# A two-layer trunk on one core: where the attention's weight loads are issued, in which order its chunks of weights are split, and how far its scores run ahead

## The chip, the cores and the metric

The kernel runs on one core of a Trainium2 chip. The metric is the device time of one execution in microseconds (us). The engines of a core work on queues of their own and in order: TensorE (PE; PEld is its loading of stationary operands), VectorE (DVE), ScalarE (ACT), GpSimd (POOL) and SyncE (SP), which here only issues transfers. Each DMA is issued from the queue of one engine; those of SP and those of POOL are two different queues of transfers (q1 and q0 in the profile).

## The reference: what is computed

A sequence of 1024 tokens with 1024 features goes through two layers. Layer 0 mixes tokens with a gated linear recurrence (RG-LRU), layer 1 with stick-breaking attention; each is followed by a SwiGLU feed-forward network of width 2816, with RMS norms before each part, and one at the end. All values are float32. The part that the change is about is the attention, 16 heads of 64:

```python
z = jnp.einsum("bhqd,bhkd->bhqk", qb, kb).astype(jnp.float32) * scale
strict = s_idx < t_idx
log_fail = jnp.where(strict, jax.nn.log_sigmoid(-z), 0.0)
suffix = lax.cumsum(log_fail, axis=3, reverse=True) - log_fail
weights = jnp.where(strict, jnp.exp(jax.nn.log_sigmoid(z) + suffix), 0.0)
outs.append(jnp.einsum("bhqk,bhkd->bhqd", weights.astype(vb.dtype), vb))
```

A query's weight on a key is sigmoid(z) of that key times the product of sigmoid(-z) over all later keys before the query. The kernel forms F = sigmoid(-z) and scans it backwards with a running product: the difference of neighbouring products is the weight, so the products themselves are multiplied with differences of neighbouring rows of V.

## The kernel before, in words

The program is straight-line: Python loops write out every instruction once. Dense products keep float32 accuracy by splitting each operand into a high and a low part (a rounded copy made by ACT, and a subtraction made by DVE) and multiplying three times. A framework allocates the tiles of a pool (a tag with `bufs` buffers), places waits, and plans the order of instructions on an engine by its own costs, except inside `manual_schedule`, where the named engines keep the order in which the code is written. The attention section is written by hand for all five engines, SP among them. The feed-forward sections are written by hand for all but SP; there the planner orders SP's transfers, and it may set instructions of neighbouring sections between one another.

Attention works on pairs of heads (`q` = 0 to 7). One pair has 24 *chunks* of scores (`chunk_list`): 128 queries by up to 512 keys. For each chunk:

- `z_part` (L1646): two matmuls into a score bank of PSUM (`psZ`, two banks).
- `z_rest` (L1658): ACT's sigmoid into a tile `w` (three buffers; diagonal chunks of j >= 4 have tiles of their own).
- `scan` (L1665): DVE's backward running product, in place. A chunk that is not on the diagonal starts from the first column of the diagonal chunk of its queries.
- `turn_weights` (L1677): ACT's copy to float16 (`wx`, four buffers), DVE's subtraction for the low half, and a transposing DMA from SP into a tile `wt` (three buffers, each for four chunks).

`score` (L1774) does this a step at a time. It issues the matmuls of chunk c, then splits and turns chunk c-1 (`turn_weights`), then the sigmoid and the scan of chunk c. So ACT's order in a step is copy of c-1, sigmoid of c; DVE's order is subtraction of c-1, scan of c.

The main loop runs over `units` u (L1704: two matmuls each of turned weights with V, called av). Chunks are `LEAD` = 8 steps ahead of units. Each step has: a chunk's score, one entry of the list `later`, one unit, and two pieces of `fill`. Fill is the projection of the next pair's Q, K and V (`qkv_steps`): three *links* per pair, each 8 steps of 6 matmuls and an evacuation (`evacuate`) per 512 tokens. K's evacuation makes t on DVE, its high part on ACT and its low part on DVE, and POOL then issues the copies into `kk` (L1636). `later` holds short jobs that are served one a step: the split of the next link's weights (`next_weights`, L1548 and L1549), the squares and norms of V's columns (`column_norms`), and for a finished pair `gather`, `add_v` (a POOL addition, L1720, except for the last pair) and `parts` (ACT L1727 and DVE L1728, then two stores issued by POOL).

Weights of Q, K, V and of the output projection are loaded by `load_link`, one link ahead of their split. These loads go to POOL's queue, as two transfers of half a tile each (L121); all other weights are loaded by SP (L117), whole. They share three buffers `raw`. POOL's queue in attention thus holds, in order: weight loads, the copies of Q and K (L1632, L1633, L1636), additions, small integer work for the norms, a memset of one column of `vt` (L1594), and the stores and returns of finished rows. At the end of the last pair `bring_back` returns the stored rows in 26 transfers (L1513, L1514).

In the feed-forward sections `Weights.a_lo` (L716) subtracts for the low part of a weight tile, and `tasks` (L1124) lists at which position of the first visits the products that come back from memory are split (`split_op`).

Of the kernel before, what the change touches and what calls it, by code (L numbers as in the profile page):

```python
# [8 lines left out]
F32 = mybir.dt.float32  # L9
F32R = mybir.dt.float32r  # L10
BF16 = mybir.dt.bfloat16
# [6 lines left out]
P = 128  # L18
# [16 lines left out]
def trunk(  # L35
# [76 lines left out]

    def load_raw(src, shape, queue=nc.sync):
        raw = rp.tile([P, D], F32, tag="raw", name="raw")
        view = raw if len(shape) == 1 else raw.rearrange("p (a b) -> p a b", a=shape[0])
        if queue is nc.sync:
            queue.dma_start(view, src)  # L117
        else:
            for i in range(2):
                c = slice(i * D // 2, (i + 1) * D // 2)  # L120
                queue.dma_start(raw[:, c].rearrange("p (k c) -> p k c", c=P), src[:, 4 * i : 4 * i + 4])  # L121
        return raw
# [37 lines left out]
    class Mix:  # L160
# [7 lines left out]

        def load(self, i, **kw):
            self.raw[i] = load_raw(cols(self.src, self.order[i] * P), (ND,), **kw)  # L170

# [459 lines left out]
    def mix_out_ffn_in(mix, bias, layer, gnext, outs):  # L631
# [42 lines left out]
        class Weights:  # L674
# [40 lines left out]

            def a_lo(self):  # L716
                lo = wtile("wal")
                V.tensor_sub(self.full(lo), self.full(self.ra), self.full(f32(self.wa)))
                self.put((0, 1), self.wa, lo)
# [57 lines left out]
        with tc.manual_schedule(engines={E.PE, E.Activation, E.DVE, E.Pool}):  # L777
# [224 lines left out]
            for k, i in enumerate(ORDER0[:6]):  # L1002
                part(P0[i], w, i, rhs_in[i], (HK - 1,))
                if k == 1:
                    w.d_hi()
                    w.d_lo()
                elif k == 3:
                    nw.a_hi()
                elif k == 5:
                    nw.a_lo()  # L1010
                if k < 5:
                    post0(i, P0[i])
# [110 lines left out]
            L = NPROD  # L1123
            tasks = [(at, p, i) for at, i in zip((2, 2, 3, 4, 5, 5, L), ORDER) for p in range(2)]  # L1124

# [72 lines left out]
            for s_, (kind, x) in enumerate(steps):  # L1198
# [24 lines left out]
                for k, i in enumerate(ORDER):  # L1223
# [18 lines left out]
                    if not final and kind == "v" and x == NV - 1:  # L1242
# [5 lines left out]
                        elif k == 5:  # L1248
                            ql = ring.four.tile([P, D], F32R, tag="w", name="wlo")
                            V.tensor_sub(ql, raw, f32(qh))  # L1250
                            k3 = lambda t: t.rearrange("p (k c) -> p k c", k=ND)
                            wq0.append((k3(qh), k3(ql)))
# [234 lines left out]
    with ExitStack() as st:  # L1487
# [3 lines left out]
        psZ = pos.enter_context(tc.tile_pool(name="psZ", bufs=2, space=PSUM, side="right", reuse_waits="tile"))  # L1491
        psN = st.enter_context(tc.tile_pool(name="psN", bufs=1, space=PSUM, reuse_waits="tile"))
        psO = st.enter_context(tc.tile_pool(name="psO", bufs=2, space=PSUM, reuse_waits="tile"))
        psQ = qs.enter_context(tc.tile_pool(name="psQ", bufs=2, space=PSUM, side="right", reuse_waits="tile"))


        unit = ap.tile([P, NB], F32, name="unit")
        nc.gpsimd.memset(unit[:, 0 : NB - P], 0.0)
# [18 lines left out]
        def load_link(i):  # L1517
            q, which = divmod(i, 3)
            if q < NP:
                raws[i] = load_raw(cols(w_qkv, which * D + q * P), (ND,), queue=nc.gpsimd)  # L1520
            else:
                mix[0].load(which, queue=nc.gpsimd)

        def column_norms(raw, q):
            sq = ap.tile([P, ND, P], BF16, tag="sq", name="sq", bufs=1)
            r3 = raw.rearrange("p (k c) -> p k c", k=ND)

            def sums():
                nc.scalar.square(sq[:, 4:], r3[:, 4:])
                n_ps = psN.tile([P, 1], F32, tag="n", name="n_ps")  # L1530
                for k in range(ND):
# [11 lines left out]

            return lambda: nc.scalar.square(sq[:, 0:4], r3[:, 0:4]), sums

# [42 lines left out]
        def evacuate(q, which, n, ps):  # L1588
            full = lambda tag, m: [ap.tile([P, m, S], F32R, tag=tag, name=tag, bufs=4 if m == 1 else 3) for _ in range(2)]
            cs = slice(n * NB, (n + 1) * NB)  # L1590
            if which == 2:
                if n == 0:
                    VT[q] = ap.tile([P, S + 1], F32, tag="vt", name="vt", bufs=2)
                    nc.gpsimd.memset(VT[q][:, 0:1], 0.0)  # L1594
                    VV[q] = ap.tile([P, 2, NT, 2, HD], F16, tag="v", name="v", bufs=2)
                t = ap.tile([P, NB], F32, tag="t", name="t", bufs=2)
                after = VT[q][:, n * NB + 1 : (n + 1) * NB + 1]
                nc.vector.scalar_tensor_tensor(after, ps, f32(sv[q]), rbc[n], op0=ALU.mult, op1=ALU.mult)
                yield
                nc.vector.tensor_sub(t, VT[q][:, cs], after)  # L1600
                vx = ap.tile([P, 4, 2, P], F16, tag="vx", name="vx", bufs=1)
                t3 = t.rearrange("p (b c) -> p b c", b=4)
# [16 lines left out]
            else:  # L1619
                t = ap.tile([P, NB], F32, tag="t", name="t", bufs=2)  # L1620
                nc.vector.tensor_mul(t, ps, rbc[n])
# [24 lines left out]
        def z_part(q, hx, j, ci, c0, c1, diag):  # L1646
            nk = (j + 1) * P
            ps = psZ.tile([P, NB], F32, tag="z", name="z_ps")
            lhsT = Q[q][hx][:, j * P : (j + 1) * P]
# [27 lines left out]
        def turn_weights(q, hx, j, ci, c0, c1, diag):  # L1677
# [6 lines left out]
            if g not in T:  # L1684
                T[g] = ap.tile([P, 8, 4, P], F16, tag="wt", name="wt", bufs=3)
            nc.sync.dma_start(
# [9 lines left out]
        def av_part(q, hx, G, kb, first, last):  # L1696
# [42 lines left out]
            if hx == 1:  # L1739
                later.extend((add_v, parts))  # L1740

        heads = [(q, hx) for q in range(NP) for hx in range(2)]
        chunks = [c for q, hx in heads for c in chunk_list(q, hx)]
        units = [u for q, hx in heads for u in unit_list(q, hx)]
        LEAD = 8

# [131 lines left out]
```

## Time and profile before

| | us |
|---|---|
| median of 3 runs | 2302.44 |
| lowest and highest run | 2298.66 and 2302.54 |
| the profiled execution | 2293.64 |
| its span, first to last instruction | 2291.9 |
| PE busy in the span | 2137.0 (93%) |
| DVE busy | 1787.2 (78%) |
| ACT busy | 1135.0 (50%) |
| POOL busy | 261.1 (11%) |

Attention runs from about 952 to 1570 us of the span. A busy PE is not PE at its peak, since matmuls are pipelined; the granted clock (PEclk, 1.00 is full) tells how fast it was allowed to run. The DMA share is the mean over 16 engines of the time that packets took, and can pass 1 where transfers of two queues overlap. In rows of waits, the name on the right is what ended the wait; in a timeline, idle time before an instruction stands in brackets with what ended it.

### The profile page before, as it was taken

How to read it: one execution, taken by the hardware profiler on the slowest of the kernel's cores; microseconds unless marked ns; L12 is line 12 of the kernel's file. 1: busy time of each engine (PE TensorE's matmuls, PEld its weight loads, DVE VectorE, ACT ScalarE, POOL GpSimd, SP SyncE). 2: the span in 40 equal slices, each digit the busy share in tenths (PEclk: the TensorE clock that was granted, in tenths of full speed). 3: DMA queues.
4: the chain of work that ended last, by engine and by line, in shares of the span. 5: the costliest groups of instructions: out<-in, count | busy, mean ns of one | idle time of the engine just before them, and what ended most of it. 6: DMA issues, size and time to landing. Idle time of an engine off the chain costs nothing.

```text
span 2291.9 us, 28023 instructions
## 1 busy us (share of the span) xinstructions
PE 2137.0 (93%) x9838; PEld 1728.4 (75%) x9838; DVE 1787.2 (78%) x2604; ACT 1135.0 (50%) x1838; POOL 261.1 (11%) x334
## 2 busy tenths in 40 slices
PE   9999999999999999987778787649999999999999
PEld 7888888888888888865556555427888888888887
DVE  7888588888887888866668766645888888878886
ACT  6676445444444455644445544434454444444556
POOL 1222010000000000122222222231100000000002
PEclk9999999999999999998999999869999999999999
DMA  6111422344447745377878877796223444477452
GB/s 222 55 37 56 156 74 92 115 138 152 139 155 266 245 140 159 124 148 151 161 155 162 158 156 151 154 193 191 74 88 113 136 156 138 152 260 259 147 154 90
DMA packets 443981, 336.45 MB, mean 147 GB/s; under 512 B 187704, under 2 KB 356800, under 8 KB 443840
## 3 DMA queue, kind: packets, MB, share of 16 engines
q1 hardware_dynamic: 427168, 281.95, 43.6%
q0 software_dynamic: 16512, 52.44, 10.1%
q8 instruction: 77, 1.26, 0.2%
q14 instruction: 64, 0.52, 0.1%
q10 hardware_dynamic: 160, 0.27, 0.0%
HBM read 184.09 MB, written 83.36 MB: 117 GB/s over the span
## 4 chain that ended last, share of the span: by engine, by line
PE 73%; DVE 10%; issue 7%; ACT 5%; DMA 4%; POOL 2%; DVEq 0%; ACTq 0%
PE p_ps L150 16%; PE p_ps L148 16%; PE p_ps L149 16%; DMA wt<-wx 4%; DVE w L1670 3%; DVE w L1673 3%; PE a_ps L149 2%; PE a_ps L150 2%; PE a_ps L148 2%; PE ob_ps L149 2%; PE ob_ps L148 2%; PE ob_ps L150 2%; ACT wx L1681 2%; ACT w L1663 2%; DVE wx L1682 1%
## 5 line engine op out<-in xcount | busy, mean ns | idle before, releaser
L148 PE MATMUL p_ps<-vh,wbh 128*128 128x512 f32 x524 | 204.9, 391 | 0.0
L149 PE MATMUL p_ps<-vl,wbh 128*128 128x512 f32 x524 | 204.5, 390 | 0.0
L150 PE MATMUL p_ps<-vh,wbl 128*128 128x512 f32 x524 | 204.3, 390 | 0.3 <-DVE wbl L727 0.3
L148 PE MATMUL p_ps<-vh,wch 128*128 128x512 f32 x524 | 204.2, 390 | 0.0
L150 PE MATMUL p_ps<-vh,wcl 128*128 128x512 f32 x524 | 204.2, 390 | 0.0
L149 PE MATMUL p_ps<-vl,wch 128*128 128x512 f32 x524 | 203.9, 389 | 0.0
L1650 PE MATMUL z_ps<-kk,q 128*128 128x256 f32 (+1 forms) x192 | 78.2, 407 | 103.0 <-ACT w L1663 92.9
L1681 ACT CAST wx<-w 128x128 f16<-128x128 f32 (+1 forms) x192 | 97.9, 510 | 152.5 <-DVE w L1670 60.6
L1682 DVE TENSOR_TENSOR wx<-w,wx 128x128 f16<-128x128 f32 (+1 forms) x192 | 107.2, 558 | 75.7 <-ACT wx L1681 72.8
L723 ACT CAST wbh<-sb 128x1024 fp32r<-128x1024 f32 (+2 forms) x69 | 69.6, 1009 | 191.7 <-DVE sb L707 191.7
L150 PE MATMUL p_ps<-vh,wal 128*128 128x512 f32 x396 | 154.3, 390 | 0.1
L148 PE MATMUL p_ps<-vh,wah 128*128 128x512 f32 x396 | 154.1, 389 | 0.0
L149 PE MATMUL p_ps<-vl,wah 128*128 128x512 f32 x396 | 154.1, 389 | 0.0
L1650 PEld LDWEIGHTS z_ps<-kk,q 128*128 128x128 f32 x192 | 38.9, 202 | 133.4 <-ACT w L1663 117.4
L148 PE MATMUL qk_ps<-vh,whi 128*128 128x512 f32 x264 | 133.5, 506 | 0.0
L223 POOL TENSOR_TENSOR acc<-acc,rbc 128x512 f32<-128x512 f32 x30 | 40.7, 1357 | 772.5 <-ACT rbc L222 772.5
L121 POOL DMA_DIRECT2D raw<-in_attn_w_qkv x46 | 35.5, 771 | 752.3 <-DVE g L1186 623.2
L1663 ACT ACTIVATE w<-z_ps,rs 128x128 f32<-128x128 f32 (+1 forms) x192 | 110.5, 575 | 15.9 <-PE z_ps L1651 15.5
L1704 PE MATMUL av_ps<-wt,v 128*128 128x512 f16 (+3 forms) x384 | 104.4, 358 | 14.9 <-DMA wt<-wx 8.8
L150 PEld LDWEIGHTS p_ps<-vh,wbl 128*128 128x128 f32 x524 | 98.4, 188 | 22.3 <-DVE wbl L727 1.5
L150 PEld LDWEIGHTS p_ps<-vh,wcl 128*128 128x128 f32 x524 | 98.4, 188 | 21.0 <-DVE wcl L737 0.6
L148 PEld LDWEIGHTS p_ps<-vh,wch 128*128 128x128 f32 x524 | 98.4, 188 | 20.5 <-ACT tb L1182 0.2
(407 smaller groups left out, 6087.4 us busy)
## 6 DMA issues: line engine op xcount, KB each, us to landing
raw<-in_ffn_w_in SPq DMA_DIRECT2D x88, 512.0 KB, 4.0
vl<-pd SPq DMA_DIRECT2D x128, 256.0 KB, 3.6
pd<-U SPq DMA_DIRECT2D x90, 256.0 KB, 2.3
kk<-two POOLq DMA_DIRECT2D x64, 256.0 KB, 5.2
raw<-in_ffn_w_out SPq DMA_DIRECT2D x56, 256.0 KB, 3.8
raw<-in_attn_w_qkv POOLq DMA_DIRECT2D x46, 256.0 KB, 3.9
h<-hd SPq DMA_DIRECT2D x32, 256.0 KB, 5.3
hd<-h SPq DMA_DIRECT2D x32, 256.0 KB, 2.0
```

Of the source, the lines that this page charges most:

```text
L148: nc.tensor.matmul(ps, lhsT=wh, rhs=mh, start=first, stop=False, **kw)
L149: nc.tensor.matmul(ps, lhsT=wh, rhs=ml, start=False, stop=False, **kw)
L150: nc.tensor.matmul(ps, lhsT=wl, rhs=mh, start=False, stop=last, **kw)
L223: (eng or nc.gpsimd).tensor_add(acc[n], acc[n], sq)
L723: nc.scalar.copy(self.full(self.wb), self.full(self.sb))
L1650: nc.tensor.matmul(ps[:, 0 : c1 - c0], lhsT=lhsT, rhs=KK[q][hx][:, 0, c0:c1], start=True, stop=False)
L1663: nc.scalar.activation(F, ps[:, 0:n], AF.Sigmoid, scale=rs[:, j : j + 1])
L1670: nc.vector.tensor_tensor_scan(rev, rev, unit[:, NB - n :][:, ::-1], 0.0, op0=ALU.mult, op1=ALU.add)
L1673: nc.vector.tensor_tensor_scan(rev, rev, rev, first, op0=ALU.mult, op1=ALU.bypass)
L1681: nc.scalar.copy(wx[:, 0:m, 0], F)
L1682: nc.vector.tensor_sub(wx[:, 0:m, 1], F, wx[:, 0:m, 0])
L1704: nc.tensor.matmul(ps[:, q0 * P :], lhsT=lhsT, rhs=rhs, start=first and part == 0, stop=last and part == 1)
```

## The change

- `load_raw` always issues one whole transfer from SP; the two halves from POOL are gone, for the weights of Q, K, V and of the output projection.
- `score` issues matmuls, sigmoid and scan of chunk c first, and then splits and turns chunk c-1. In a step ACT's order is now sigmoid of c, copy of c-1; DVE's is scan of c, subtraction of c-1.
- Scores have four banks: a pool `psY` of two beside `psZ`, taken in turn. The bank of its own for the norms (`psN`) is gone; the norms take a score bank.
- `LEAD` is 10 instead of 8, and `wt` has four buffers instead of three.
- The squares of the norms (`sq`) and V's halves (`vx`) share the tag and the four buffers of `wx`. `t` has one buffer instead of two, and `unit`, an operand of the diagonal scans, is BF16 instead of float32.
- The two squares of the norms are two entries of `later` instead of the second being made right before the norm's matmuls; and an empty entry stands between `add_v` and `parts`.
- Outside attention: two subtractions for low parts are made in two pieces (the first weights of the second step of each feed-forward section, and the first weights of Q, there in the order in which the first link reads them), and two products are split one or two positions later in `tasks`.

```diff
-    def load_raw(src, shape, queue=nc.sync):
+    def load_raw(src, shape):
         raw = rp.tile([P, D], F32, tag="raw", name="raw")
         view = raw if len(shape) == 1 else raw.rearrange("p (a b) -> p a b", a=shape[0])
-        if queue is nc.sync:
-            queue.dma_start(view, src)
-        else:
-            for i in range(2):
-                c = slice(i * D // 2, (i + 1) * D // 2)
-                queue.dma_start(raw[:, c].rearrange("p (k c) -> p k c", c=P), src[:, 4 * i : 4 * i + 4])
+        nc.sync.dma_start(view, src)
         return raw
...
-            def a_lo(self):
+            def a_lo(self, parts=1):
                 lo = wtile("wal")
-                V.tensor_sub(self.full(lo), self.full(self.ra), self.full(f32(self.wa)))
+                if parts == 1:
+                    V.tensor_sub(self.full(lo), self.full(self.ra), self.full(f32(self.wa)))
+                else:
+                    for x in range(2):
+                        V.tensor_sub(self.part(lo, x), self.part(self.ra, x), self.part(f32(self.wa), x))
                 self.put((0, 1), self.wa, lo)
...
                 elif k == 5:
-                    nw.a_lo()
+                    nw.a_lo(2)
...
-            tasks = [(at, p, i) for at, i in zip((2, 2, 3, 4, 5, 5, L), ORDER) for p in range(2)]
+            tasks = [(at, p, i) for at, i in zip((2, 2, 3, 4, 5, L, L + 1), ORDER) for p in range(2)]
...
                             ql = ring.four.tile([P, D], F32R, tag="w", name="wlo")
-                            V.tensor_sub(ql, raw, f32(qh))
+                            ka = lambda t: t.rearrange("p (a k c) -> p a k c", a=2, k=HK)
+                            for y in (slice(1, 3), slice(0, HK, HK - 1)):
+                                V.tensor_sub(ka(ql)[:, :, y], ka(raw)[:, :, y], ka(f32(qh))[:, :, y])
...
-        psN = st.enter_context(tc.tile_pool(name="psN", bufs=1, space=PSUM, reuse_waits="tile"))
+        psY = st.enter_context(tc.tile_pool(name="psY", bufs=2, space=PSUM, reuse_waits="tile"))
+        taken = []
+
+        def z_bank(name):
+            taken.append(name)
+            return (psZ, psY)[len(taken) % 2].tile([P, NB], F32, tag="z", name=name)
...
-        unit = ap.tile([P, NB], F32, name="unit")
+        unit = ap.tile([P, NB], BF16, name="unit")
...
-                raws[i] = load_raw(cols(w_qkv, which * D + q * P), (ND,), queue=nc.gpsimd)
+                raws[i] = load_raw(cols(w_qkv, which * D + q * P), (ND,))
             else:
-                mix[0].load(which, queue=nc.gpsimd)
+                mix[0].load(which)
...
-            sq = ap.tile([P, ND, P], BF16, tag="sq", name="sq", bufs=1)
+            sq = ap.tile([P, ND, P], BF16, tag="wx", name="sq", bufs=4)
...
-                nc.scalar.square(sq[:, 4:], r3[:, 4:])
-                n_ps = psN.tile([P, 1], F32, tag="n", name="n_ps")
+                n_ps = z_bank("n_ps")[:, 0:1]
...
-            return lambda: nc.scalar.square(sq[:, 0:4], r3[:, 0:4]), sums
+            squared = lambda i: nc.scalar.square(sq[:, 4 * i : 4 * i + 4], r3[:, 4 * i : 4 * i + 4])
+            return lambda: squared(0), lambda: squared(1), sums
...
-                t = ap.tile([P, NB], F32, tag="t", name="t", bufs=2)
+                t = ap.tile([P, NB], F32, tag="t", name="t", bufs=1)
...
-                vx = ap.tile([P, 4, 2, P], F16, tag="vx", name="vx", bufs=1)
+                vx = ap.tile([P, 4, 2, P], F16, tag="wx", name="vx", bufs=4)
...
-            ps = psZ.tile([P, NB], F32, tag="z", name="z_ps")
+            ps = z_bank("z_ps")
...
-                T[g] = ap.tile([P, 8, 4, P], F16, tag="wt", name="wt", bufs=3)
+                T[g] = ap.tile([P, 8, 4, P], F16, tag="wt", name="wt", bufs=4)
...
             if hx == 1:
-                later.extend((add_v, parts))
+                later.extend((add_v, lambda: None, parts))
...
-        LEAD = 8
+        LEAD = 10
...
         def score(some):
-            ps = [z_part(*a) for a in some]
+            for a in some:
+                z_rest(z_part(*a), *a)
+                scan(*a)
             while turning:
                 turn_weights(*turning.pop(0))
-            for a in some:
-                z_rest(ps.pop(0), *a)
-                scan(*a)
-                turning.append(a)
+            turning.extend(some)
```

More of the change, by code (lines that the diff above doesn't have):

```diff
@@ L167, in __init__, with load @@
                 self.proc(i)
-        def load(self, i, **kw):
-            self.raw[i] = load_raw(cols(self.src, self.order[i] * P), (ND,), **kw)
+        def load(self, i):
+            self.raw[i] = load_raw(cols(self.src, self.order[i] * P), (ND,))
         def proc(self, i):
@@ L1619, in evacuate @@
             else:
-                t = ap.tile([P, NB], F32, tag="t", name="t", bufs=2)
+                t = ap.tile([P, NB], F32, tag="t", name="t", bufs=1)
                 nc.vector.tensor_mul(t, ps, rbc[n])
```

## The prediction

> **What bounds the kernel now.** First the page's head and the windows, to find the stage that loses time.
>
> ```profile
> span 2291.9 us, 28023 instructions
> ...
> core 0: us, PE busy (x) PEld busy (x) DVE busy (x) ACT busy (x) POOL busy (x), PEclk, DMA share, GB/s
> 160.00:900.00 740.00, 739.93 (x3433) 618.67 (x3432) 606.54 (x854) 358.64 (x539) 28.85 (x15) 1.00 0.45 144
> 1000.00:1500.00 500.00, 392.34 (x1735) 280.25 (x1733) 355.58 (x519) 244.35 (x478) 135.86 (x224) 0.92 0.80 156
> 1500.00:1570.00 70.00, 40.47 (x145) 24.40 (x145) 34.94 (x46) 22.72 (x43) 14.16 (x20) 0.73 0.97 183
> 1146.00:1216.00 70.00, 54.59 (x245) 39.08 (x244) 50.39 (x75) 34.46 (x68) 19.02 (x31) 0.95 0.79 158
> ```
>
> Outside attention PE is busy 739.93 of 740 us: nothing to win there. In 1000:1500 nobody is full: PE 392 of 500 us, DVE 356, ACT 244, DMA 0.80. One pair of heads (24 chunks of scores) lasts 70 us, with 50.4 us of DVE. So I read next who waits, engine by engine, in 1000:1500.
>
> ```profile
> engine line waited for: us in total, times, longest us
> DVE oo L1728 <- ACT oh L1727: 70.2, 7, 13.8
> DVE wx L1682 <- ACT wx L1681: 41.7, 61, 1.2
> DVE w L1673 <- ACT w L1663: 15.5, 7, 3.0
> DVE vx L1604 <- ACT vx L1603: 9.7, 14, 0.7
> ACT oh L1727 <- POOL oo L1720: 72.2, 7, 14.3
> ACT wx L1681 <- DVE w L1670: 51.4, 83, 1.7
> ACT wx L1681 <- DVE w L1673: 48.5, 42, 2.3
> PE z_ps L1650 <- ACT w L1663: 59.0, 30, 12.9
> PE n_ps L1532 <- ACT sq L1529: 25.3, 7, 4.5
> PE av_ps L1704 <- DMA wt<-wx: 8.8, 8, 1.6
> POOL raw L121 <- issue: 86.9, 23, 6.5
> ```
>
> DVE is idle for 500 - 355.6 = 144.4 us; its four rows add to 137.1. That is the whole account: DVE and ACT hold each other up, PE waits behind them (59.0). The timeline shows the two mechanisms.
>
> ```profile
> 1185.88 0.68 ACT L1663 ACTIVATE w<-z_ps,rs 128x512 f32<-128x512 f32 x1
> 1186.01 0.69 DVE L1682 TENSOR_TENSOR wx<-w,wx 128x512 f16<-128x512 f32 x1 [1.21 <-ACT wx L1681]
> 1186.62 1.28 DVE L1673 TENSOR_TENSOR_SCAN w<-w,w 128x512 f32<-128x512 f32 x1
> 1187.92 0.62 ACT L1681 CAST wx<-w 128x512 f16<-128x512 f32 x1 [1.37 <-DVE w L1673]
> ...
> 1189.04 2.44 POOL L1636 DMA_DIRECT2D kk<-two  x4 [9.31 <-ACT w L1663]
> 1192.92 0.79 POOL L121 DMA_DIRECT2D raw<-in_attn_w_qkv  x1 [1.44 <-issue]
> 1199.52 0.75 POOL L121 DMA_DIRECT2D raw<-in_attn_w_qkv  x1 [5.81 <-issue]
> 1200.29 1.10 POOL L1720 TENSOR_TENSOR oo<-oo,vt 128x512 f32<-128x512 f32 x1
> ...
> 1201.43 0.72 ACT L1727 ACTIVATE oh<-oo,av 128x512 fp32r<-128x512 f32 x1 [9.25 <-POOL oo L1720]
> ```
>
> Mechanism one: POOL's add sits in order behind a weight load whose second half gets out 5.81 us late, ACT stands 9.25 us before its scaling of that sum, and everything behind ACT stands too. Mechanism two: ACT's copy of chunk c-1 comes ahead of its sigmoid of chunk c, and needs the scan of c-1; so sigmoid, scan and copy run one after another (0.68 + 1.28 + 0.62).
>
> **The change, part by part.**
>
> *Loads to SyncE.* The add then follows its input, and gets one more step before ACT asks for it. Gain: the first DVE row, 70.2 us. The first pair has the same stall once, through the memset of vt behind a load:
>
> ```profile
> 992.64 0.75 POOL L121 DMA_DIRECT2D raw<-in_attn_w_qkv  x1 [5.78 <-issue]
> 993.38 0.12 POOL L1594 MEMSET vt<- 128x1 f32 x1
> ...
> 994.25 0.63 ACT L1603 ACTIVATE vx<-t 128x512 f16<-128x512 f32 x1 [6.54 <-DVE t L1600]
> ```
>
> That is 6.5 more. For this part a rule speaks against the gain. The Trainium skill (DMA: Bandwidth & Descriptors, section SWDGE vs HWDGE vs iDMA, "Issuing engines are not separate DMA queues") says that spreading issues over engines saves only the issuing time. By that rule these 77 us would not come back, since an issue is short. The trace disagrees: 86.9 us of waits before 23 POOL loads, none of them the 0.75 us of the issue itself.
>
> On SP the loads stand among the transposes. Their raw buffer was last read a link (8 steps) earlier, so SP does not wait for it; what is queued behind is transposes, costed below. At the start of the stage load 1 may fall behind the last stores of the residual on SP: between 0 and 5 us, I take 0, because the planner may place ACT's first split by arrival.
>
> *Split a scan later.* Sigmoid c no longer stands behind the scan of c-1, and copy c-1 finds its scan done. Gain at most the 41.7 us of the second DVE row. *Squares a step earlier and four banks:* PE reaches its norm matmuls with both halves squared, and scores can be four chunks ahead of the sigmoid; gain at most the 15.5 us of the third row (25.3 on PE are no path of their own). The 9.7 of vx stay. The new order's own needs: sigmoid c takes the w buffer of chunk c-3, which the subtraction of c-3 has freed a step earlier on DVE, so it does not wait; the norm's result takes one of the four score banks for a moment; and the four banks that the next section opens now come free with the last scores instead of standing empty, up to 1 us, which I leave at nothing. LEAD 10 adds two steps in which PE multiplies without new scores at the end and two without products at the start: the same instructions, spread otherwise.
>
> Sum of gains: 70.2 + 6.5 + 41.7 + 15.5 = 133.9 us.
>
> **What is late next.** Four things, each from a row:
>
> ```profile
> 1183.69 0.39 PE L1650 MATMUL z_ps<-kk,q 128*128 128x512 f32 x1
> ...
> 1191.72 0.39 PE L1650 MATMUL z_ps<-kk,q 128*128 128x512 f32 x1
> ACT two L1624 <- DVE t L1621: 29.5, 14, 2.3
> kk<-two POOLq DMA_DIRECT2D x56, 256.0 KB, 5.8
> raw<-in_ffn_w_in SPq DMA_DIRECT2D x88, 512.0 KB, 4.0
> DMA to landing us min/median/max: 2.3/4.0/8.5
> DMA to landing us min/median/max: 2.5/10.4/17.7
> ACT wx L1681 <- DMA wt<-wx: 32.0, 7, 11.9
> L1670 DVE TENSOR_TENSOR_SCAN w<-w,unit x114: 416/825/1227, 999.7 to 1498.0; 128x256 f32<-128x256 f32 x29, 128x384 f32<-128x384 f32 x29, 128x512 f32<-128x512 f32 x28, 128x128 f32<-128x128 f32 x28
> L718 DVE TENSOR_TENSOR wal<-raw,wah x70: 684/1218/1222, 307.6 to 2263.0; 128x1024 fp32r<-128x1024 f32 x58, 128x768 fp32r<-128x768 f32 x8, 128x512 fp32r<-128x512 f32 x4
> ```
>
> (The two landing lines are the transposed tiles wt, first in 1000:1480, then in 1490:1545; the wait for wt is that of 1000:1600; the scans are those of 1000:1500.)
>
> 1. K evacuations. ACT's cast waits for DVE's t in the same step, and the next sigmoid stands behind it: 0.62 + 0.68 = 1.3 us of DVE idle, 14 times: 18 us.
> 2. K's copies. Two issues of 2.44/4 each and 5.8 us to land, then score and sigmoid (0.39 + 0.68): 8.1 us before chunk 28, the first that reads the second half of the next pair's K, can be scanned. DVE has three steps of work until then, at 50.4/24 = 2.1 us each 6.3: 1.8 x 7 = 13 us.
> 3. PE. Four steps take 1191.72 - 1183.69 = 8.03 us, 24 take 48 us, against DVE's 50: two nearly full engines with three or four chunks between them. Between 0 and 3 us a pair, I take 1.5: 10 us.
> 4. Shared buffers. Squares and vx now take one of the four buffers of wx. From copy to landing it is 0.62 + 1.28 + 0.69 + 4.0 = 6.6 us; three buffers cover 3 x 2.1 = 6.3, four cover 8.4. Between 0 and 2 us a pair, I take 1: 7 us.
>
> Together 48 us come back. Net: 133.9 - 48 = 86 us.
>
> At nothing: LEAD 10 with four wt tiles (av waited 8.8 us in all, and the slack before an av goes from 4 steps to 6); the last pair, where the bringing back of stored rows floods the DMA and ACT waits for transposes (most of the 32.0 us) as before, between 5 us less and 10 more; unit in BF16, where no row shows a scan with a BF16 operand: 114 scans of about 0.825 us, 5% either way is 5 us, I take none; the split subtractions before the FFN (2 x 0.684 against 1.218, 0.15 us more DVE) and the splits of two products, one or two positions later, both under a PE that is never short there: up to 1 us if that cover went.
>
> The profiled execution took 2293.64 us around its 2291.9; the median of the runs is 2302.44, 8.8 more. 2293.64 - 86 = 2207.6, and against the median 2302.4 - 86 = **2216 us**.
>
> **The rivals.**
>
> *Floor.* Nothing comes back: 2302.4 - 134 = 2168. For it: POOL's add is the only long stall. Against: point 1 is in the order of the program.
>
> *DMA paces it.* At a share of 0.80, and if the mean cannot pass 0.90, 500 us shrink by 56: 2246. For it: 0.97 with DMA waits in 1500:1570. Against: there it is large transfers from one queue.
>
> *Loads ahead of transposes.* A transpose behind a load waits for it: it lands at 4.0 + 4.0 = 8.0 us, where four buffers at 2.1 us a step, less 2.6 for copy, scan and subtraction, cover 5.8. 2.2 us x 24 loads = 53: 2302.4 - 86 + 53 = 2269. The Trainium skill (DMA: Bandwidth & Descriptors, section Queues, rings and completion order) supports this: an engine takes turns between queues packet by packet, but serves one queue in its order, so a load loses its place beside the transposes and gets one ahead of them. No run so far shows it.
>
> *Loads not the cause.* Without the loads' 77 us: 134 - 77 - 48 = 9: 2293.
>
> *Slower.* The same place as the third rival, at the price of the flooded stretch: transposes behind each load land at 10.4 us, 4.6 over the cover, x 24 = 110 us: 2302.4 - 86 + 110 = 2326. It decides from a landing of 5.8 + 86/24 = 9.4 us on. For it: 10.4 was measured. Against: that took 26 transfers in a row, not one every 23 us.
>
> **How the numbers follow.** Forecast 0.48 (its own range 2185 to 2250), floor 0.12, DMA 0.10, loads ahead of transposes 0.14, loads not the cause 0.04, slower 0.12. The range 2160 to 2290 leaves out the slower case, most of the fourth and the deepest floor: about 2 in 10. 0.2% is 4.6 us, about what a measurement of this kernel can tell from no change. Faster: 0.83; within it 0.03; slower 0.14, with a little for what no row shows.
>
> **What would show it.** ACT's wait for POOL's oo gone, under 10 us in all; DVE wx <- ACT wx under 10; PE n_ps <- ACT sq near nothing; DVE busy above 0.83 in the stage, PE's clock in it near 1.00; a pair in 57 to 60 us. The fourth point is right if ACT waits some 7 us for wt before the last pair. Wrong would be: ACT wx <- DMA wt in the tens before the last pair (loads ahead of transposes); the stall at oo surviving with POOL waiting on K's or the rows' own transfers; PE waiting for kk by more than 3 us a pair.

## The result, and the profile after

The changed kernel takes 2295.84 us (median of 18 runs, 2287.69 to 2306.09); the kernel before, beside it, 2299.27 us. The ratio is 0.9989 with an interval of 0.9976 to 1.0003: no change that these runs can tell from none. The forecast was 2216 us, its range 2160 to 2290. Some 80 us are missing.

From the page of the changed kernel, the span, its two large DMA queues (packets, MB, share) and the chain that ended last:

```profile
span 2292.9 us, 28073 instructions
...
q1 hardware_dynamic: 454208, 295.58, 48.6%
q0 software_dynamic: 12352, 38.81, 7.9%
...
PE 76%; DMA 12%; DVE 6%; issue 2%; ACT 2%; SPq 0%; POOL 0%; DVEq 0%; ACTq 0%
```

The last three of these on the page of the kernel before:

```profile
q1 hardware_dynamic: 427168, 281.95, 43.6%
q0 software_dynamic: 16512, 52.44, 10.1%
...
PE 73%; DVE 10%; issue 7%; ACT 5%; DMA 4%; POOL 2%; DVEq 0%; ACTq 0%
```

The loads have left POOL's queue (q0), and 12% of the chain is now a DMA, where it was 4%. The windows of the changed kernel, for the stage of attention that the prediction was worked out in, and for a stall and the stretch behind it:

```profile
core 0: us, PE busy (x) PEld busy (x) DVE busy (x) ACT busy (x) POOL busy (x), PEclk, DMA share, GB/s
1000.00:1500.00 500.00, 385.05 (x1708) 283.94 (x1707) 340.71 (x509) 235.71 (x468) 99.95 (x182) 0.88 0.93 157
1118.00:1130.00 12.00, 7.03 (x28) 5.46 (x29) 4.15 (x6) 1.26 (x3) 0.81 (x1) 0.86 1.18 137
1130.00:1160.00 30.00, 29.40 (x139) 21.73 (x138) 28.19 (x44) 19.50 (x40) 7.50 (x13) 1.00 0.85 164
```

DVE is busy for 340.7 of the 500 us, where it was 355.6. Who waits for whom, in 1000:1500 of the changed kernel (engine, line, what it waited for: us, times, longest):

```profile
DVE vx L1610 <- ACT vx L1609: 80.6, 13, 19.9
DVE w L1679 <- ACT w L1669: 59.6, 22, 6.0
DVE w L1676 <- ACT w L1669: 9.1, 8, 1.3
DVE wx L1688 <- ACT wx L1687: 7.6, 6, 3.0
ACT vx L1609 <- DMA wt<-wx: 111.2, 13, 22.4
ACT sq L1549 <- DMA wt<-wx: 37.0, 7, 6.7
ACT wx L1687 <- DMA wt<-wx: 22.1, 14, 3.6
PE n_ps L1537 <- ACT sq L1549: 57.5, 14, 8.2
PE z_ps L1656 <- DMA kk<-two: 35.0, 7, 5.7
```

Both stalls that the change aims at are gone: no row of ACT waiting for POOL's `oo` is left, and DVE's wait for the copy (41.7 us before) is 7.6. In their place ACT waits 111.2 + 37.0 + 22.1 = 170 us for transposes, to write V's halves, the squares and the chunks' copies: the three users of the shared ring of four. DVE's four rows add to 156.9 us, against 137.1 before. One stall in the timeline of the changed kernel (start, length, engine, line, tiles; idle time before in brackets):

```profile
1112.27 0.62 ACT L1687 CAST wx<-w 128x512 f16<-128x512 f32 x1 [0.57 <-DVE w L1679]
...
1114.08 2.40 POOL L1642 DMA_DIRECT2D kk<-two  x4 [9.50 <-ACT wx L1687]
1114.13 0.57 SPq L116 DMA_DIRECT2D raw<-in_attn_w_qkv  x1
1114.80 11.49 SPq L1692 DMA_TRANSPOSE wt<-wx  x4
...
1116.80 0.50 ACT L1687 CAST wx<-w 128x384 f16<-128x384 f32 x1
...
1117.72 1.09 POOL L1726 TENSOR_TENSOR oo<-oo,vt 128x512 f32<-128x512 f32 x1 [1.13 <-DVE oo L1722]
1118.34 1.56 DVE L1676 TENSOR_TENSOR_SCAN w<-w,unit 128x512 f32<-128x512 f32 x1
...
1120.87 0.68 DVE L1606 TENSOR_TENSOR t<-vt 128x512 f32<-128x512 f32 x1
...
1128.74 0.63 ACT L1609 ACTIVATE vx<-t 128x512 f16<-128x512 f32 x1 [11.44 <-DMA wt<-wx]
1129.40 0.69 DVE L1610 SCALAR_TENSOR_TENSOR vx<-t,vx 128x512 f16<-128x512 f32 x1 [7.85 <-ACT vx L1609]
```

The copy at 1112.27 fills a buffer, SP issues a weight load at 1114.13, and the first transpose behind it at 1114.80; POOL has begun to issue K's copies at 1114.08. ACT comes to V's halves at 1117.30, behind its copy of 1116.80. Their input `t` is there at 1121.55, but all four buffers of the ring are still in use, and they start at 1128.74. So of the 11.44 us some 4 are a wait for `t`, and 7 for the ring. By the ends of `t` in the trace it is 39 of the 111.2 us in all; the other 72 and 13 copies of 0.63 make up DVE's row of 80.6. In the 12 us from 1118 on DVE works for 4.15 us; in the 30 us behind the stall it works for 28.19. So the loop of chunks runs at the speed that the prediction asked for, and loses it again at such places. From issue to landing of the transposed tiles of the changed kernel, in 1000:1480 and in 1105:1132:

```profile
DMA to landing us min/median/max: 2.3/4.5/15.0
DMA to landing us min/median/max: 3.1/9.1/13.9
```

Before, the first was 2.3/4.0/8.5. The median has hardly moved; the late ones are later. The 13.9 us are those of the transpose at 1114.80: it lands just before V's halves start.

### The profile page after: what moved, and what is told of

It is laid out like the page before. It is cut to its first block, busy times and chain, and to the rows that moved or that the text cites. A ratio compares the mean times of both kernels' runs of the same rounds, so it can differ in the third digit from the quotient of the medians.

```text
span 2292.9 us, 28073 instructions
## 1 busy us (share of the span) xinstructions
PE 2135.3 (93%) x9838; PEld 1737.4 (76%) x9838; DVE 1778.3 (78%) x2607; ACT 1131.0 (49%) x1838; POOL 220.3 (10%) x282
## 3 DMA queue, kind: packets, MB, share of 16 engines
q1 hardware_dynamic: 454208, 295.58, 48.6%
q0 software_dynamic: 12352, 38.81, 7.9%
## 4 chain that ended last, share of the span: by engine, by line
PE 76%; DMA 12%; DVE 6%; issue 2%; ACT 2%; SPq 0%; POOL 0%; DVEq 0%; ACTq 0%
PE p_ps L143 17%; PE p_ps L145 17%; PE p_ps L144 17%; DMA wt<-wx 11%; PE a_ps L144 2%; PE a_ps L145 2%; PE a_ps L143 2%; PE ob_ps L145 2%; PE ob_ps L143 2%; PE ob_ps L144 2%; DVE w L1676 1%; PE i_ps L145 1%; PE i_ps L144 1%; PE i_ps L143 1%; DVE wx L1688 1%
## 5 line engine op out<-in xcount | busy, mean ns | idle before, releaser
L1679 DVE TENSOR_TENSOR_SCAN w<-w,w 128x512 f32<-128x512 f32 x64 | 81.9, 1279 | 59.8 <-ACT w L1669 59.6
L1676 DVE TENSOR_TENSOR_SCAN w<-w,unit 128x128 f32<-128x128 f32 (+3 forms) x128 | 106.6, 833 | 11.6 <-ACT w L1669 11.6
```

The lines of the kernel that those rows point to most:

```text
L1676: nc.vector.tensor_tensor_scan(rev, rev, unit[:, NB - n :][:, ::-1], 0.0, op0=ALU.mult, op1=ALU.add)
L1679: nc.vector.tensor_tensor_scan(rev, rev, rev, first, op0=ALU.mult, op1=ALU.bypass)
```

## The experiments

Each time is a median beside runs of the kernel before on the same chip (2298.4 to 2300.6 us in the five groups of runs); each ratio is to those, with its interval. Windows lie at fixed times: in 1000:1500 a faster kernel has come further towards the end of attention, where transposes land late before the change too (10.4 us in the median in 1490:1545), so 1000:1400 is the fairer one.

### Undone in the changed kernel: the sharing, or the queue

**Own buffers for squares and V's halves** (and three `wt`, to make room):

```diff
-sq = ap.tile([P, ND, P], BF16, tag="wx", name="sq", bufs=4)
+sq = ap.tile([P, ND, P], BF16, tag="sq", name="sq", bufs=1)
-vx = ap.tile([P, 4, 2, P], F16, tag="wx", name="vx", bufs=4)
+vx = ap.tile([P, 4, 2, P], F16, tag="vx", name="vx", bufs=1)
```

> The changed kernel with buffers of their own for the squares and for vx again (one each), paid for with wt back at three buffers; LEAD stays 10. Theory A (the shared buffers are the new stall: ACT's vx waited 111.2 us and its squares 37.0 us for a buffer that a transpose still held): both rows fall under 10 us, DVE goes above 0.78 in 1000:1500, time 2200 to 2240. Theory B (the loads on SP hold the transposes up): the wait comes back at wx itself, ACT wx <- DMA wt rises from 22 to 60 us or more, time 2260 to 2300. Theory C (the DMA engines are full at a share of 0.93): time within 10 us of 2296, share unchanged, the waits only change their names.

2260.09 us, 0.9841 (0.9819 to 0.9863). With loads on SP the sharing costs 36 us. Both rows of the ring are gone, as theory A asked, but the wait has moved to the chunks' copies, as theory B asked, and is smaller; ACT's wait in 1000:1400 of this kernel, where the changed kernel's three rows have 119.5 us:

```profile
ACT wx L1687 <- DMA wt<-wx: 65.1, 20, 7.5
```

**Loads back on POOL's queue**, in two halves as before:

```diff
-raws[i] = load_raw(cols(w_qkv, which * D + q * P), (ND,))
+raws[i] = load_raw(cols(w_qkv, which * D + q * P), (ND,), queue=nc.gpsimd)
```

> The changed kernel with the attention's weight loads on POOL again, in halves; all else as changed. A: the waits of vx and squares for a buffer stay within a third of 148 us, and POOL's add is late again: 2300 to 2340. B: transposes land as before (4.0 us median, 8.5 at most before the last pair), vx and squares wait under 40 us together; the stall at the add is partly covered by its extra step: 2240 to 2290. C: DMA share stays above 0.9, time 2290 to 2310.

2281.28 us, 0.9924 (0.9897 to 0.9950): in the changed kernel, loads on SP are 15 us worse than loads on POOL. The old stall is back in a new place, on V's first column, whose memset stands behind a load on POOL. DVE's waits in 1000:1400 of this kernel, and the landing of its transposes there:

```profile
DVE t L1611 <- POOL vt L1605: 20.2, 5, 5.9
DMA to landing us min/median/max: 2.3/4.9/13.9
```

Theory B asked for landings as before (8.5 us at most). They are late here too, with no load of these weights in SP's queue.

**Loads as 128 rows of 4 KB**, the same number of bytes, of other weights (so the kernel computes something else):

```diff
-raws[i] = load_raw(cols(w_qkv, which * D + q * P), (ND,))
+raws[i] = load_raw(w_qkv[q * P : (q + 1) * P, which * D : (which + 1) * D].rearrange("p (a b) -> p a b", a=1), (1,))
```

> The changed kernel with each weight load of Q, K and V taken as 128 rows of 4 KB instead of 1024 pieces of 512 bytes (the same bytes, issued from SP at the same place; the weights are the wrong ones, so the output is not the reference's). A: no change beyond 10 us. B or C by way of the small pieces: transposes behind a load land sooner, maximum below 10 us before the last pair, DMA share of the SP queue falls from 0.63 towards 0.5, time 2240 to 2280.

2280.19 us, 0.9925 (0.9903 to 0.9948). Longer rows are worth 16 us of 80; the shape of the load isn't the main thing. The latest transpose in 1000:1400 still lands after 15.2 us, where a maximum below 10 was expected.

### What in SP's queue does it, with own buffers

Four kernels, each with one change to the kernel with own buffers: **loads on ACT's queue**, so that neither POOL's additions nor SP's transposes stand behind them; **six buffers `wx`**; **no loads** from link 5 on (of links 0 to 23; the last weights loaded are used again, so the output is another); and **transposes of the high halves alone** (the products read them twice, and the output is another):

```diff
+raws[i] = load_raw(..., queue=nc.scalar)                      # first
-wx = ap.tile([P, 4, 2, P], F16, tag="wx", name="wx", bufs=4)
+wx = ap.tile([P, 4, 2, P], F16, tag="wx", name="wx", bufs=6)  # second
+if i <= 4:                                                    # third
+    kept_raw[:] = [load_raw(cols(w_qkv, which * D + q * P), (ND,))]
+raws[i] = kept_raw[0]
-    T[g][:, 0 : 2 * m, j % 4], wx[:, 0:m].rearrange("p b h c -> p (b h c)"), transpose=True
+    T[g][:, 0:m, j % 4], wx[:, 0:m].rearrange("p b h c -> p (b h c)")[:, 0 : m * P], transpose=True  # fourth
```

> The first run (own buffers for squares and vx, three wt) with the attention's weight loads issued whole from ACT: a third queue, so that they stand neither before POOL's add nor before SP's transposes. B (order in SP's queue is what holds the transposes up): ACT wx <- DMA wt falls from 93 us to under 30 in 1000:1480, time 2200 to 2230. C (the DMA engines are the limit, whatever the queue): the wait stays at 70 us or more, time 2250 to 2270.

> The first run with six buffers of wx instead of four, loads on SP. If the transposes are late only in bursts (behind a load, beside K's copies), two more steps of cover (4 us) take most of the wait: ACT wx <- DMA wt under 30 us, time 2215 to 2240. If the DMA engines cannot keep the pace on average (C), the backlog only grows longer: the wait stays above 60 us, time 2245 to 2262.

> The first run without the weight loads of links 5 and later: those links split and use the tile of link 4 again (the output is not the reference's; 19 or 20 loads of 512 KB are left out, everything else stays). If the loads on SP are what makes the transposes late (B), ACT wx <- DMA wt falls under 25 us and the time to 2195 to 2225. If K's and Q's copies from POOL are (the rest of the DMA work), it stays above 50 us and the time above 2240.

> The first run with only the high half of each chunk's weights turned (half the bytes of every wt transpose; av multiplies it twice, so the output is not the reference's; the subtraction on DVE stays). C: with a quarter of the DMA work gone, the waits for wt go under 20 us and the time falls to 2190 to 2220, below what any other queue for the loads gives. B: transposes still stand behind loads, the wait falls by less than half, 2230 to 2255.

Against the 2260 of own buffers alone: ACT's queue 2223.48 (0.9679, 0.9659 to 0.9700), six buffers 2212.62 (0.9630, 0.9611 to 0.9650), no loads 2214.77 (0.9645, 0.9617 to 0.9674), half the transposed bytes 2225.29 (0.9683, 0.9659 to 0.9707). So the loads cost 45 us in that kernel, and 37 of it go when they leave SP's queue. ACT's wait for transposes doesn't go with them: of 65.1 us in 1000:1400, 43.5 are left with the loads on ACT's queue and 35.1 without loads, more than was expected of either. And the DMA engines aren't the limit, which was the rival "DMA paces it": with six buffers the share is higher and the time lower. The windows of the kernel with six buffers, and after it ACT's wait for transposes in the same 400 us:

```profile
1000.00:1400.00 400.00, 354.83 (x1628) 262.22 (x1627) 328.10 (x486) 229.78 (x448) 97.09 (x163) 0.95 1.02 179
```

```profile
ACT wx L1687 <- DMA wt<-wx: 9.7, 9, 2.0
```

The transposes still land late (in 1000:1400 12.7 us at the latest against 15.2, median 4.8 against 5.1), but two more buffers let ACT go on: 9.7 us in place of 65.1.

What makes a transpose late where no load is? The kernel without loads tells. First the landing of its transposes in 1020:1370, where it loads no weights, and the same of the kernel with own buffers; then K's copies at one place, and the transpose that SP issues 1.1 us behind the first of them:

```profile
DMA to landing us min/median/max: 2.3/3.8/11.4
DMA to landing us min/median/max: 2.3/5.1/15.2
```

```profile
1204.69 2.34 POOL L1646 DMA_DIRECT2D kk<-two  x4 [5.97 <-issue]
DMA to landing us min/median/max: 11.3/11.3/11.3
```

So transposes beside K's copies land late, up to 11.4 us, with no load at all; the loads raise the median from 3.8 to 5.1 and the longest to 15.2.

### One part alone in the kernel before

**The loads on SP alone, the order of the split alone, the loads on ACT's queue alone, and these last two together:**

```diff
-raws[i] = load_raw(cols(w_qkv, which * D + q * P), (ND,), queue=nc.gpsimd)
+raws[i] = load_raw(cols(w_qkv, which * D + q * P), (ND,))                   # SP
+raws[i] = load_raw(cols(w_qkv, which * D + q * P), (ND,), queue=nc.scalar)  # ACT
...
-ps = [z_part(*a) for a in some]
+for a in some:              # the order
+    z_rest(z_part(*a), *a)
+    scan(*a)
 while turning:
     turn_weights(*turning.pop(0))
-for a in some:
-    z_rest(ps.pop(0), *a)
-    scan(*a)
-    turning.append(a)
+turning.extend(some)
```

> The kernel before with one part alone: its weight loads of attention issued whole from SP. My prediction's account: the 70 us of DVE's wait at the add go, time 2225 to 2245. B: the transposes wait behind loads, ACT wx <- DMA wt rises from 2 us to 40 or more in 1000:1500, time 2265 to 2300. C: DMA share goes from 0.80 to 0.9 and the time falls by 30 us at most, 2270 to 2300.

> The kernel before with one part alone: sigmoid and scan of chunk c ahead of the split of chunk c-1 (loads stay on POOL, two score banks, LEAD 8). My prediction's term for it was at most 41.7 us: DVE wx <- ACT wx falls from 41 to under 10, time 2258 to 2275. If the two score banks or POOL's add take the gain (the stall of 70 us stays, and PE must have the next scores ready a step sooner), DVE w <- ACT w rises instead: 2280 to 2300.

> The kernel before with one part alone, its loads issued whole from ACT instead of POOL: neither POOL's add nor SP's transposes have them ahead. My prediction's term for freeing POOL was 70.2 + 6.5 us. If that term was right and only the queue chosen took it back (from SP it was 26 us), 2222 to 2240. If DVE's wait at the add was largely cover for other waits that now show, 2250 to 2275 as from SP.

> The kernel before with loads on ACT and the split a scan later, the rest as before (two score banks and one for the norms, LEAD 8, three wt, own buffers, no empty entry in later). My term for the order was up to 41.7 us on top. If it is there once POOL and SP are free of loads, 15 to 40 us below the run before it; if four banks and LEAD 10 are needed to use it, within 8 us of it.

Loads on SP: 2273.13 us, 0.9894 (0.9862 to 0.9926), 26 us. Loads on ACT's queue: 2239.44, 0.9735 (0.9710 to 0.9760), 61 us. Freeing POOL's addition is thus worth most of the predicted 77, and SP's queue takes 34 of that back, even with squares and V's halves in buffers of their own. DVE's waits with the loads on ACT's queue, in 1000:1400:

```profile
DVE wx L1682 <- ACT wx L1681: 39.4, 57, 1.4
DVE w L1673 <- ACT w L1663: 13.0, 6, 3.0
DVE vx L1604 <- ACT vx L1603: 9.1, 13, 0.7
```

The row of `oo` has gone and the other three stand as they were before (34.6, 12.5 and 7.7 in the same 400 us): just the account of the prediction, less its first row.

The order alone: 2288.39, 0.9936 (0.9912 to 0.9960), some 12 us of the 41.7; its ten runs spread from 2270.80 to 2306.47. On top of the loads on ACT's queue it costs, which neither theory allowed: 2260.05, 0.9809 (0.9750 to 0.9868), 21 us more than without it by the medians. Its four runs spread from 2240.52 to 2270.07 and the two intervals just touch, so the size is rough. The waits of all engines in 1000:1400 of this last kernel say why:

```profile
DVE w L1670 <- ACT w L1663: 54.4, 34, 3.3
DVE wx L1682 <- ACT wx L1681: 11.9, 11, 2.0
ACT w L1663 <- PE z_ps L1651: 84.5, 55, 4.0
PE av_ps L1704 <- DMA wt<-wx: 41.8, 14, 4.9
```

The wait that the order removes (39.4 to 11.9) comes back: chunks are turned a step later, so PE waits for them before its products with V (41.8, where it was 12.0), its next scores come late, the sigmoid waits for them (84.5, was 13.0), and the scan for the sigmoid (54.4). With two banks and a lead of 8 the order has no cover on PE's side. Four banks and a lead of 10, taken alone, were not tried.

### The queue, or the cover

In the changed kernel: **a shared ring of eight** (and three `wt`) with the loads on SP; **loads on ACT's queue** with the shared ring of four; and with own buffers, **both cures** (six `wx` and ACT's queue).

```diff
-sq = ap.tile([P, ND, P], BF16, tag="wx", name="sq", bufs=4)    # and vx, wx
+sq = ap.tile([P, ND, P], BF16, tag="wx", name="sq", bufs=8)    # and vx, wx
...
+raws[i] = load_raw(cols(w_qkv, which * D + q * P), (ND,), queue=nc.scalar)
```

> The changed kernel with the shared ring of wx, vx and squares at eight buffers, paid for with wt at three: the same memory as six of wx and one each of the others, which took 2212.6 us. If what costs is how many steps of cover the ring has (theory A as a matter of number), 2208 to 2222. If sharing itself costs, because a square or a vx takes its turn behind a late transpose and stands ahead of everything else on ACT, 2235 to 2260.

> The changed kernel, shared ring of four as it is, with the loads on ACT's queue. If queue and sharing act apart, the gain is that of the separate buffers, 36.6 us: 2255 to 2265. If the ring of four is short with or without loads ahead of the transposes, less: 2268 to 2290. If the loads ahead of the transposes were all that emptied the ring, more: 2225 to 2245.

> Own buffers, six of wx, and the loads on ACT's queue: the two cures together. Alone they took 2212.6 (six) and 2223.5 (ACT), from 2260.1. If both cure the same late transposes, little is left: 2200 to 2213. If the loads also cost something of their own (DMA engines' time, PE's wait for K's copies), 2185 to 2200.

Ring of eight: 2215.07 us, 0.9623 (0.9583 to 0.9664), 81 us under the changed kernel. ACT's queue: 2228.13, 0.9690 (0.9673 to 0.9708), 68 under it. Both: 2218.34, 0.9648 (0.9625 to 0.9670), above both expectations and no better than more buffers alone. So the two cures are for one loss. Sharing itself is no loss: the ring of eight shares too. With the loads on ACT's queue, shared (2228) and own buffers (2223) differ by 5 us.

ACT's waits for transposes with the ring of eight, in 1000:1500 and in 1000:1400, then with the loads on ACT's queue in 1000:1500:

```profile
ACT wx L1687 <- DMA wt<-wx: 32.8, 7, 10.6
ACT wx L1687 <- DMA wt<-wx: 0.3, 1, 0.3
```

```profile
ACT wx L1692 <- DMA wt<-wx: 63.1, 31, 9.0
ACT sq L1554 <- DMA wt<-wx: 19.3, 6, 4.3
ACT vx L1614 <- DMA wt<-wx: 16.7, 4, 5.2
```

With the ring of eight next to nothing is left before 1400. Of V's 111.2 us, 16.7 are left when the loads leave the queue, and 13.5 of these are the wait for `t`. The transposes land at 10.4 us at the latest in 1000:1400, where it was 15.0, and at 18.8 behind 1460, near the end of attention.

Leaving the queue isn't the only thing that changes for the load. Where K's copies go out, in the changed kernel, SP issues it within 0.1 us of them (1114.13 and 1114.08 above); ACT issues it 4.3 us ahead:

```profile
1107.39 0.37 ACTq L117 DMA_DIRECT2D raw<-in_attn_w_qkv  x1
1111.72 2.40 POOL L1647 DMA_DIRECT2D kk<-two  x4 [9.51 <-ACT wx L1692]
```

So the 68 us, like the 37 with own buffers, are the price of the queue and of the moment together, and no run holds one and changes the other.

### The load cut in four

In the changed kernel, **each load of Q, K and V weights in four pieces, one a step**; then the same with **the ring of eight**:

```diff
+return [lambda s=slice(2 * x, 2 * x + 2): nc.sync.dma_start(view[:, s], src[:, s]) for x in range(4)]
...
+if pieces and done % 2 == 0:
+    pieces.pop(0)()
+done += 1
```

> The changed kernel with each 512 KB load of Q, K and V weights issued by SP in four pieces of 128 KB, one a step over four steps, in place of one whole; same bytes, same 512-byte packets, same queue, ring of four as in the changed kernel. Known: the same kernel with the loads on ACT's queue gains 68 us, with eight buffers 81. Theory burst (a transpose waits for the bytes that stand before it in SP's queue, and only what passes the ring's cover costs): no transpose stands behind more than a quarter load at a time, the longest landing falls from 15 to under 9 us, ACT's waits for wt in 1000:1500 fall from 170 to under 80, time 2230 to 2260. Theory total (what counts is the sum of load bytes in the queue of the transposes, however cut): landing median rises, maxima fall, the waits stay at 130 or more, time 2280 to 2300. Theory issues (each DMA issued by SP before a transpose costs SP or the queue a fixed time): four times as many, time 2300 or more.

> The changed kernel with the shared ring of eight (and three wt tiles) and the loads cut into four pieces as in the run before. The ring of eight alone gave 2215. Theory burst: the ring of eight covers the burst already, so cutting adds nothing: 2208 to 2220. Theory total: the pieces keep more transposes late, 2215 to 2230.

2269.88 us, 0.9870 (0.9845 to 0.9896): 26 us better than the changed kernel, between what the theories of the burst (2230 to 2260) and of the sum of the bytes (2280 to 2300) asked for; that of a price for each issue is out, since four times as many issues made the kernel faster. The longest landing in 1000:1400 is still 13.5 us, where the burst asked for under 9. With the ring of eight: 2216.23, 0.9658 (0.9625 to 0.9692), the same as without cutting. ACT's waits for transposes in 1000:1500 of the first:

```profile
ACT vx L1624 <- DMA wt<-wx: 82.5, 12, 19.0
ACT wx L1702 <- DMA wt<-wx: 32.8, 16, 5.2
ACT sq L1556 <- DMA wt<-wx: 31.5, 6, 6.2
```

147 us are left of 170. Where V's halves are due, all four pieces still fall into the stretch in which K's copies move too: they are issued from 1112.28 to 1121.95 at one such place, the copies from 1112.22, and the last of these lands at 1123.83. The kernel without loads shows that transposes are late beside such copies; how much of this stall is theirs is open, since no run moved them.

## Why the prediction was wrong

**The step that failed** is point 4, "Shared buffers", with its "Between 0 and 2 us a pair, I take 1: 7 us", together with the loads on SP, for which the prediction named the transposes as queued behind and then took no price in its sum. The bound took the median landing of 4.0 us for every transpose. The median did stay near it (4.5 us). But the ring fails by its latest transposes: 13.9 us for the one behind the load at 1114, at the very place where V's halves ask for a fifth buffer while four copies hold theirs. In place of 7 us, with loads on SP, the sharing costs 36 (2296 to 2260), and the loads in SP's queue 37 more of what is left (2260 to 2223); taken in the other order, queue first, it is 68 and 5. The two can't be priced one by one. Together it is some 73 to 81 us, about what is missing.

**The rival that came nearest** in mechanism is "loads ahead of transposes", at 2269 us and with a chance of 0.14. Late transposes that empty a ring of four are what the runs show; that the load's place in the queue is what makes them late is a part of it, beside K's copies and the moment of the load. Its price of 53 us was too low: 68 (by the queue) to 81 (by the cover). It also had the shape wrong. It spread 2.2 us over 24 loads, all at the chunks' copies. The trace has one long wait a pair at V's halves (11.44 us in the timeline, 22.4 the longest), seven at the squares of 37.0 / 7 = 5.3, and only 22.1 us at the copies. The Trainium skill (DMA: Bandwidth & Descriptors, section Queues, rings and completion order) says that a queue is served in its order. The runs agree in part: with another queue 68 us come back (at another moment), and with the same bytes in the same queue, cut in four, 26. Why the rest stays when the load is cut is open.

**The other rivals.** "Loads not the cause" gives 2293 us, closest of all to the time measured, and is refuted, so that its number is luck: moving the loads alone gains 26 us on SP and 61 on ACT's queue. "Slower" is the same place at a price of 110 us; it would have decided from 86 us on, and the price came to 68 to 81, so it stayed just short of it. "DMA paces it" falls with the shares above 1. The floor of 2168 was reached by no run.

**The loads off POOL** (70.2 + 6.5) were right in kind: 61 us with a queue that holds nothing else, and 26 on SP. The Trainium skill's rule that spreading issues over engines saves only the issuing time (DMA: Bandwidth & Descriptors, section SWDGE vs HWDGE vs iDMA, "Issuing engines are not separate DMA queues") would have this at next to nothing, since it calls that time usually small. The runs differ: 61 us for another issuing engine and one whole transfer in place of two halves. What came back is what stood behind the loads on POOL.

**The split a scan later** (41.7 at most): the wait went to 7.6 as forecast, but alone it is worth 12, and with two banks and a lead of 8 it costs 21 beside free loads. "PE reaches its norm matmuls with both halves squared" is wrong too: PE's wait for the squares rose from 25.3 to 57.5, because the squares wait for a buffer of the ring; with the ring of eight that row is gone. All parts of the change but the loads' queue, measured under the loads on ACT's queue (2239 to 2228), are worth 11 us, where the prediction had 41.7 + 15.5 less 48 = 9. That is near, but the order and the shared buffers, two of its terms, came out otherwise, and no run shows the rest, so the agreement may be luck.

**K's copies** (13 us): PE waits 35.0 us for `kk` in the changed kernel, 5.0 a pair, over the 3 that the prediction gave as a sign of error. With the ring of eight it is 12.4 in the same 500 us, with own buffers, six `wx` and the loads on ACT's queue 38.8, though ACT waits only 16.0 us for transposes in 1000:1400 there; so the stall of the ring doesn't explain this row, and what sets it is open. **K's evacuations** and **PE's coupling** are not told apart by any run.

**Taken at nothing.** `unit` in BF16 was right: the shorter diagonal scans take 952, 682 and 416 ns in the changed kernel (958, 689 and 418 before). Those of 512 take 1291 in the mean (1223 before), but not for their operand: six of the 28 in 1000:1500 run beside POOL's addition and take 1555 to 1562, as the one of 1.56 us at 1118.34 in the timeline does, and the others take 1206 to 1225.

**The signs.** Of those named, "ACT wx <- DMA wt in the tens" came true as the sign of error; DVE busy above 0.83 did not (340.7 / 500 = 0.68), nor PE's clock near 1.00 (0.88), nor a pair in 57 to 60 us. Outside attention nothing moved by more than 2 us: the first sigmoid starts at 984.5 us before and 986.4 after, the last at 1560.7 and 1560.9, of spans of 2291.9 and 2292.9.

From the ring of eight and the six buffers, 2215 and 2213 us, it can be seen that the forecast's 2216 is about what this change gives when the transposes have cover; that its other terms are right one by one doesn't follow. These two kernels are the fastest of all here, 3.7 to 3.8% under the kernel before.

## What to carry to other kernels

Price a ring of buffers by the latest transfer that holds one, not by the median (here 13.9 us against 4.5), and look for the place where two users take from it in one step. Before a load goes to a queue, list which short transfers stand behind it and how many steps of cover they have: here a 512 KB load a link in the queue of the transposes cost 68 us in all, and a ring of eight instead of four, for one `wt` less, hid it. A wait that disappears from its row isn't a gain until the engine's idle time has shrunk: here DVE's rows went from 137 to 157 us while both of the targets were gone.

## What the hardware showed that was not expected

- The same 26 weight loads (13.63 MB) make 454208 - 427168 = 27040 packets more on SP's queue and 16512 - 12352 = 4160 fewer on POOL's: 1040 a load, of some 0.5 KB, against 160, of some 3.3 KB. These are the numbers of the two pages under the result. On SP, 4 KB rows in place of 512-byte ones were worth 16 us.
- A DMA share of 1 and more is no limit by itself: at 1.00 to 1.07 in 1000:1400 the kernels with more buffers were faster than the changed kernel at 0.92. In its stall it was 1.18 with only 137 GB/s moved, less than the 164 GB/s of the stretch behind it at 0.85.
- The diagonal scan of 512 takes 1206 to 1225 ns, and 1555 to 1562 where it runs beside an addition on POOL (six of 28 in the changed kernel; none of the 28 before, whose additions fall elsewhere).
